# Latent attention in a two-layer fp32 block: the rope's halves swapped by ScalarE, the softmax issued later, the score passes regrouped

## The chip, the cores and the metric

The kernel runs on one core of one Trainium2 chip. The metric is the device time of one execution in microseconds. The profile shows one execution, with its span (first to last instruction) and the granted clock of TensorE as a share of full speed (2.4 GHz; the lower level is 1.2 GHz).

## The reference

A sequence of 512 tokens of width 1024 passes two layers. The first has an attention with forget gates ("fox"), the second a latent attention ("MLA") with 16 heads, and each is followed by a feed-forward part with a short convolution. The change is in the latent attention:

```python
def apply_rope(x, cos, sin):
    x1, x2 = jnp.split(x, 2, axis=-1)
    return jnp.concatenate([x1 * cos - x2 * sin, x1 * sin + x2 * cos], axis=-1)

# shared keys and values: latent (256), one rotated key (64) for all heads
ckv = rmsnorm(x, kv_in_g) @ w_dkv
latent = rmsnorm(ckv[..., :KV_LORA], kv_norm_g)
k_rope = apply_rope(ckv[..., KV_LORA:], cos, sin)
k_nope = latent @ w_uk            # 16 heads of 128
v = latent @ w_uv                 # 16 heads of 128
# queries: 16 heads of 128 + 64 rotated
q = rmsnorm(h @ w_dq, q_norm_g) @ w_uq
sc = (q_nope @ k_nope.T + q_rope @ k_rope.T) * scale
sc = where(visible in chunks of 64, sc, -inf)
o = softmax(sc) @ v
```

All is in fp32.

## The kernel before

Every product is made of parts: an operand is kept as a high part in TensorE's fp32r format and a low part (the rest), and `mm3` issues three passes, high by high, high by low, low by high (lines 84, 85, 86). A pass streams up to 512 columns. The work is written in Python and unrolled; a scheduler orders each engine's queue, mostly as in the text, but an instruction that is ready earlier can go ahead of an earlier one that is not. Buffers rotate in pools, and an instruction waits until its buffer is free. The weights of a projection go through `load_w`: a DMA on SP's queue, a cast to the high part on ScalarE (L105) and a subtraction for the low part on POOL or VectorE (L106). Three raw buffers and two of each part stand ready.

PSUM has eight banks: three in the pool `acc` for projections and outputs, five in the pool `att` for scores and transposes. A bank is evacuated by a ScalarE operation for the high part and a VectorE operation for the low part (`split_ps`, L641 and L642).

Before the head loop the kernel projects the queries' latents (six tiles, `qc`), the rotated key (`krt`) and the keys' latents (two tiles), normalises them (`latents`, L628 and L190), and makes the rope part of the queries for heads 0 and 1 (`mm_rope(0)`), the plain queries of heads 0 and 1, the rotated key's high and low part (`mr`, L742 and L743) and the keys of heads 0 and 1.

The head loop runs over 16 heads, with the scores of head h+1 made while head h is finished. Two heads share one rope projection and one value projection, so the work comes in pairs:

- Even head: scores of the next head (20 passes, L208: per query tile of 128 rows three passes for the plain part and two for the rotated part, against 128, 256, 384 or 512 keys); `mm_rope` for the next pair (18 passes); `proj_v` (24 passes of 256 columns, L687 to L689, four tiles, each evacuated by L690 on ScalarE and L691 on VectorE); `turn`, the rotation; `attn_pT`, ten transposes of the current head's weights (L227), evacuated by L230 on ScalarE and L231 on VectorE; `split_rot`, the two parts of the rotated queries `tr` (L666 ScalarE, L667 VectorE); one key projection (6 passes); `mvalues` (12 passes, L709, of which the last four need the low halves of the transposes).
- Odd head: scores of the next head, a query projection, transposes, a key projection, a second query projection, values.

The softmax of a score tile is in the same function as its passes: a VectorE operation adds the mask and finds the row's maximum (L211), ScalarE makes the exponentials with their sum (L213), and VectorE scales by the reciprocal (L215, L217). `rope` swaps the two halves of each rotated group of 64 rows while it multiplies: four products of 32 partitions, one on POOL and three on VectorE (L637), with the cosine product on POOL (L634) and the sum on VectorE (L638).

Of the kernel before, what the change touches and what calls it, by code (L numbers as in the profile page):

```python
# [42 lines left out]
ROPE_POOL = (0,)  # L43
# [3 lines left out]
def tile_kernel(ctx, tc, xT_d, gains_d, bf_d, const_d, conv_d, wv_d, wq_d, wk_d, wfo_d,  # L47
# [31 lines left out]
    def f(ap):  # L79
        return ap.bitcast(F32)  # L80
# [116 lines left out]
    def attn_scores(p_pool, passes, mask):  # L197

        nm = T(p_pool, [P, NT], F32, "nm", 2)
        l = T(p_pool, [P, NT], F32, "l", 2)  # L200
        rl = T(p_pool, [P, 16], F32, "rl", 2)[:, :NT]
        es = []
        for i in range(NT):
            n = (i + 1) * P
            s_ps = att()
            mms = passes(i, n)
            for j, (lt, rt) in enumerate(mms):
                pe.matmul(s_ps[:, :n], lt, rt, start=(j == 0), stop=(j == len(mms) - 1))  # L208

            e = T(p_pool, [P, n], F32, f"e{i}", 2)  # L210
            v.tensor_tensor_reduce(out=e, in0=s_ps[:, :n], in1=mask[:, S - n:], scale=-1.0, scalar=BIG,  # L211
                                   op0=ALU.add, op1=ALU.min, accum_out=nm[:, i:i + 1])
            a.activation(e, e, AF.Exp, scale=-1.0, bias=nm[:, i:i + 1], accum_out=l[:, i:i + 1])  # L213
            es.append(e)
        v.reciprocal(rl, l)  # L215
        for i in range(NT):
            v.tensor_scalar(out=es[i], in0=es[i], scalar1=rl[:, i:i + 1], scalar2=None, op0=ALU.mult)  # L217
        return es
# [172 lines left out]
    with tc.tile_pool(name="fx", bufs=1, reuse_waits="tile") as fp:  # L391
# [150 lines left out]
        def scores(h):  # L542
            (t1, t2), (m1, m2) = qs.pop(h), ks.pop(h)

            def passes(i, n):
                sl = slice(i * P, (i + 1) * P)
                return [(t1[:, sl], m1[:, :n]), (t2[0:68, sl], m2[0:68, :n])]

            return attn_scores(fp, passes, mask)
# [60 lines left out]
    with tc.tile_pool(name="ml", bufs=1, reuse_waits="tile") as mp:  # L610
# [19 lines left out]

        def rope(A):

            c, t_ = r2(), r2()
            g.tensor_tensor(out=c, in0=A, in1=cosT, op=ALU.mult)  # L634
            for i in range(4):
                o, x = slice(32 * i, 32 * i + 32), slice(32 * (i ^ 1), 32 * (i ^ 1) + 32)
                (g if i in ROPE_POOL else v).tensor_tensor(out=t_[o], in0=A[x], in1=sinT[x], op=ALU.mult)  # L637
            v.tensor_tensor(out=A, in0=c, in1=t_, op=ALU.add)  # L638

# [16 lines left out]
        def turn(pt):  # L656
            A = r2()
            a.activation(A, pt, AF.Copy, scale=MSCALE)
            rope(A)
            return A  # L660
# [33 lines left out]
        def mscores(h):  # L694
# [7 lines left out]
            return attn_scores(mp, passes, mask)  # L702
# [19 lines left out]
        krt = r2()  # L722
# [4 lines left out]
        latents(0, KQ - 2, Rq, G_Q)  # L727
        down(wdkv_d[1], G_KVIN, qc[:, KQ + 1, :])
# [6 lines left out]
        pt = mm_rope(0)  # L735
# [3 lines left out]
        split_rot(0, turn(pt))  # L739
        proj_q(1)  # L740
        rope(krt)
        a.copy(mr[:, 0, :], krt)  # L742
        v.tensor_tensor(out=mr[:, 1, :], in0=krt, in1=f(mr[:, 0, :]), op=ALU.subtract)  # L743
# [17 lines left out]
        es = {0: mscores(0)}  # L761
        proj_k(2)
        proj_q(2)
        for h in range(MH):
            more = h + 2 < MH
            if h + 1 < MH:
                es[h + 1] = mscores(h + 1)
            if h % 2 == 0:
                if more:
                    pt = mm_rope(h // 2 + 1)  # L770
                proj_v(h // 2)
                if more:
                    A = turn(pt)
            elif more:
                proj_q(h + 2)
# [4 lines left out]
            if more and h % 2 == 0:  # L780
                split_rot(h // 2 + 1, A)
            if h + 3 < MH:
                proj_k(h + 3)
                if h % 2:
                    proj_q(h + 3)
# [9 lines left out]
def _constants():  # L795
# [12 lines left out]
    c[:, C_SIN:C_SIN + S] = np.concatenate([sin, -sin] * 2)  # L808
# [72 lines left out]
```

## Time and profile before

| | us |
|---|---|
| median of 3 runs | 1429.17 (1429.05 to 1430.08) |
| the profiled execution | 1429.15 |
| its span | 1427.1 |
| TensorE busy in the span | 1384.2 |
| VectorE busy in the span | 902.9 |
| ScalarE busy in the span | 636.5 |
| POOL busy in the span | 310.6 |

The granted clock is 0.983 over the span. Matmuls are pipelined, and their busy time counts overlaps, so the distance between the starts of two passes tells more than the length of one. The profile's chain of waits follows back from the last instruction what released each step; its lines give the start of a piece, its length and its work.

### The profile page before, as it was taken

Reading aid. Unit: us, or ns where it says so; the run is one execution under the profiler, and the core shown is the slowest. Engines: PE = TensorE matmul, PEld = TensorE weight load, DVE = VectorE, ACT = ScalarE, POOL = GpSimd, SP = SyncE. Lnnn points to the kernel's source line nnn. Section 1 sums busy time; section 2 is a strip of 40 time slices with the busy share of each in tenths; the row PEclk is TensorE's granted clock in tenths of the full one; section 3 lists DMA queues with packets and bytes.
Section 4 is the critical chain, followed back from the end, with each engine's and each line's share of the span. In section 5 each row is a group of like instructions: output and inputs, shape, how many; then the busy total and the mean of one; then the engine's idle time right before and its main releaser. Section 6 shows DMA issues by size and latency. Waiting matters only on the chain.

```text
span 1427.1 us, 17362 instructions
## 1 busy us (share of the span) xinstructions
PE 1384.2 (97%) x6594; PEld 1162.8 (81%) x6594; DVE 902.9 (63%) x1495; ACT 636.5 (45%) x1103; POOL 310.6 (22%) x228
## 2 busy tenths in 40 slices
PE   7999999899999999999799999999999999999997
PEld 7888887788888888888678888888888888888886
DVE  6667786677776744445876666665557777774333
ACT  5588884254444432223454555543225444442111
POOL 4333322400000002154533333321310000000222
PEclk9999999999999999999999999999999999999998
DMA  5321112222323233332111111212232323323331
GB/s 178 102 76 61 51 51 68 89 96 96 103 90 104 89 92 97 106 105 80 50 49 48 59 49 52 61 54 89 89 104 89 104 91 101 98 94 93 96 97 69
DMA packets 41251, 120.22 MB, mean 84 GB/s; under 512 B 5552, under 2 KB 9952, under 8 KB 41168
## 3 DMA queue, kind: packets, MB, share of 16 engines
q1 hardware_dynamic: 39184, 117.00, 25.8%
q0 software_dynamic: 1840, 2.09, 0.6%
q8 instruction: 51, 0.84, 0.2%
q14 instruction: 32, 0.26, 0.1%
q10 hardware_dynamic: 144, 0.03, 0.0%
HBM read 116.74 MB, written 2.36 MB: 83 GB/s over the span
## 4 chain that ended last, share of the span: by engine, by line
PE 85%; DVE 8%; ACT 3%; issue 3%; DMA 1%; POOL 1%; SPq 0%; DVEq 0%; POOLq 0%; ACTq 0%
PE acc L84 24%; PE acc L86 23%; PE acc L85 23%; PE att L208 6%; DVE r L637 2%; PE acc L556 1%; PE att L227 1%; PE acc L709 1%; DVE r L638 1%; DVE ptl L231 1%; DVE big L190 1%; ACT whi L105 1%; DVE tr L667 1%; PE att L84 1%; PE att L86 1%
## 5 line engine op out<-in xcount | busy, mean ns | idle before, releaser
L86 PE MATMUL acc<-big,wlo 128*128 128x512 f32 (+1 forms) x1504 | 584.9, 389 | 7.5 <-POOL wlo L106 3.9
L84 PE MATMUL acc<-big,whi 128*128 128x512 f32 (+1 forms) x1504 | 587.5, 391 | 3.1 <-ACT big L189 2.2
L85 PE MATMUL acc<-big,whi 128*128 128x512 f32 (+1 forms) x1504 | 584.5, 389 | 0.3 <-DVE big L190 0.3
L105 ACT CAST whi<-raw 128x1024 fp32r<-128x1024 f32 (+4 forms) x243 | 229.3, 944 | 427.7 <-PE acc L85 267.5
L86 PEld LDWEIGHTS acc<-big,wlo 128*128 128x128 f32 x1504 | 283.8, 189 | 67.9 <-POOL wlo L106 5.8
L84 PEld LDWEIGHTS acc<-big,whi 128*128 128x128 f32 x1504 | 283.7, 189 | 61.0 <-ACT big L189 2.8
L85 PEld LDWEIGHTS acc<-big,whi 128*128 128x128 f32 x1504 | 283.8, 189 | 58.2 <-DVE big L190 0.6
L106 DVE TENSOR_TENSOR wlo<-raw,whi 128x1024 fp32r<-128x1024 f32 (+3 forms) x179 | 236.2, 1320 | 141.0 <-ACT whi L105 138.3
L142 POOL TENSOR_TENSOR r<-xT 128x512 f32<-128x512 f32 x28 | 31.4, 1124 | 735.9 <-DVE xT L254 414.5
L106 POOL TENSOR_TENSOR wlo<-raw,whi 128x768 fp32r<-128x768 f32 (+3 forms) x64 | 111.8, 1749 | 223.1 <-ACT whi L105 197.3
L294 DVE SCALAR_TENSOR_TENSOR c<-u,conv,c 128x510 f32<-128x510 f32 (+1 forms) x176 | 131.1, 747 | 3.5 <-ACT c L292 0.6
L289 DVE TENSOR_TENSOR u<-acc,R 128x512 f32<-128x512 f32 x88 | 60.3, 687 | 76.3 <-PE acc L86 76.3
L213 ACT ACTIVATE e<-e,nm 128x128 f32<-128x128 f32 (+3 forms) x128 | 71.3, 557 | 43.1 <-DVE nm L211 42.1
L146 POOL TENSOR_TENSOR r<-r,r 128x512 f32<-128x512 f32 x38 | 72.1, 1898 | 27.7 <-ACT r L140 21.0
L292 ACT ACTIVATE c<-u,conv 128x512 f32<-128x512 f32 x88 | 71.4, 813 | 3.1 <-DVE u L289 2.7
L298 ACT ACTIVATE sg<-c 128x512 f32<-128x512 f32 x44 | 27.8, 632 | 78.9 <-DVE c L294 78.8
L231 DVE TENSOR_TENSOR ptl<-att,pth 128x512 fp32r<-128x512 f32 (+3 forms) x128 | 55.4, 481 | 3.4 <-ACT pth L230 2.6
L186 ACT CAST big<-sg 128x512 fp32r<-128x512 f32 x32 | 19.9, 621 | 81.7 <-DVE sg L299 81.6
L230 ACT CAST pth<-att 128x512 fp32r<-128x512 f32 (+3 forms) x128 | 46.9, 435 | 4.8 <-PE att L227 4.3
L208 PE MATMUL att<-kn,tn 128*128 128x128 f32 (+2 forms) x192 | 47.7, 364 | 0.0
L217 DVE TENSOR_SCALAR e<-e,rl 128x128 f32<-128x128 f32 (+3 forms) x128 | 43.0, 399 | 1.1
L254 DVE TENSOR_TENSOR xT<-acc,xT 128x512 f32<-128x512 f32 x20 | 13.8, 691 | 42.5 <-PE acc L86 42.5
(180 smaller groups left out, 1563.8 us busy)
## 6 DMA issues: line engine op xcount, KB each, us to landing
raw<-in_wfi SPq DMA_DIRECT2D x88, 512.0 KB, 3.5
raw<-in_wfu SPq DMA_DIRECT2D x32, 512.0 KB, 3.5
raw<-in_wmo SPq DMA_DIRECT2D x16, 512.0 KB, 3.6
raw<-in_wfu SPq DMA_DIRECT2D x16, 384.0 KB, 3.1
raw<-in_wuqn SPq DMA_DIRECT2D x16, 384.0 KB, 3.0
raw<-in_wq SPq DMA_DIRECT2D x8, 512.0 KB, 3.5
raw<-in_wk SPq DMA_DIRECT2D x8, 512.0 KB, 3.4
raw<-in_wv SPq DMA_DIRECT2D x8, 384.0 KB, 3.1
```

Of the source, the lines that this page charges most:

```text
L84: pe.matmul(out, wh, xh, start=start, stop=False)
L85: pe.matmul(out, wh, xl, start=False, stop=False)
L86: pe.matmul(out, wl, xh, start=False, stop=stop)
L105: a.copy(hi[:, c], raw[:, c])
L106: (eng or v).tensor_tensor(out=lo[:, c], in0=raw[:, c], in1=f(hi[:, c]), op=ALU.subtract)
L146: (adder or g).tensor_tensor(out=self.sum, in0=self.sum, in1=sq, op=ALU.add)
L208: pe.matmul(s_ps[:, :n], lt, rt, start=(j == 0), stop=(j == len(mms) - 1))
L213: a.activation(e, e, AF.Exp, scale=-1.0, bias=nm[:, i:i + 1], accum_out=l[:, i:i + 1])
L231: v.tensor_tensor(out=lo, in0=pt[:, :w], in1=f(hi), op=ALU.subtract)
L289: v.tensor_tensor(out=u, in0=pt, in1=R, op=ALU.mult)
L292: a.activation(c, u, AF.Identity, scale=cw[:, 2:3], bias=cw[:, 3:4])
L294: v.scalar_tensor_tensor(out=c[:, s:], in0=u[:, :S - s], scalar=cw[:, 2 - s:3 - s], in1=c[:, s:], op0=ALU.mult, op1=ALU.add)
```

## The change

Four things are changed.

- The rotation: the halves are swapped by four ScalarE copies of 32 partitions each, out of the PSUM bank of the rope projection into SBUF (`swapped`). VectorE multiplies the bank by the cosine with the scale, and later the swapped tile by the sine and adds the two. POOL has no part in it. `turn` returns a function `end`, which issues the last two operations. For the rotated key, the copies are from SBUF and the two products and the sum are on POOL; they are issued between two projections of the keys' latents, and the key's two parts (POOL for the low one) follow before the first rope projection. The key and its swapped copy lie in a buffer of the pool `kn`.
- The order in the loop: at an even head `mm_rope` and the first part of `turn` come before the next head's scores, and `proj_v` and `end` come after the transposes.
- The softmax is split off `attn_scores`: the mask and maximum of all four tiles stay with the scores, and the exponentials, the reciprocal and the scaling are issued behind the transposes of the current head. In the first layer's attention the same function is called right away.
- The passes: the four score tiles are opened at once. In the latent attention the plain passes of all four tiles come first and the rotated passes of all four after them.

```diff
@@ attn_scores
-        es = []
+        es, pts = [], [att() for _ in range(NT)]
+        for i, j, first, last, lt, rt in passes():
+            pe.matmul(pts[i][:, :(i + 1) * P], lt, rt, start=first, stop=last)
         for i in range(NT):
             n = (i + 1) * P
-            s_ps = att()
-            mms = passes(i, n)
-            for j, (lt, rt) in enumerate(mms):
-                pe.matmul(s_ps[:, :n], lt, rt, start=(j == 0), stop=(j == len(mms) - 1))
             e = T(p_pool, [P, n], F32, f"e{i}", 2)
-            v.tensor_tensor_reduce(out=e, in0=s_ps[:, :n], in1=mask[:, S - n:], scale=-1.0, scalar=BIG,
+            v.tensor_tensor_reduce(out=e, in0=pts[i][:, :n], in1=mask[:, S - n:], scale=-1.0, scalar=BIG,
                                    op0=ALU.add, op1=ALU.min, accum_out=nm[:, i:i + 1])
-            a.activation(e, e, AF.Exp, scale=-1.0, bias=nm[:, i:i + 1], accum_out=l[:, i:i + 1])
             es.append(e)
-        v.reciprocal(rl, l)
-        for i in range(NT):
-            v.tensor_scalar(out=es[i], in0=es[i], scalar1=rl[:, i:i + 1], scalar2=None, op0=ALU.mult)
-        return es
+
+        def softmax():
+            for i in range(NT):
+                a.activation(es[i], es[i], AF.Exp, scale=-1.0, bias=nm[:, i:i + 1], accum_out=l[:, i:i + 1])
+            v.reciprocal(rl, l)
+            for i in range(NT):
+                v.tensor_scalar(out=es[i], in0=es[i], scalar1=rl[:, i:i + 1], scalar2=None, op0=ALU.mult)
+
+        return es, softmax
+
+    def by_tile(of, order=None):
+        every = [of(i, (i + 1) * P) for i in range(NT)]
+        m = len(every[0])
+        for js in (order or (range(m),)):
+            for i in range(NT):
+                for j in js:
+                    yield (i, j, j == 0, j == m - 1, *every[i][j])
@@ rotation
-        def rope(A):
-            c, t_ = r2(), r2()
-            g.tensor_tensor(out=c, in0=A, in1=cosT, op=ALU.mult)
+        def swapped(dst, src, sc):
             for i in range(4):
                 o, x = slice(32 * i, 32 * i + 32), slice(32 * (i ^ 1), 32 * (i ^ 1) + 32)
-                (g if i in ROPE_POOL else v).tensor_tensor(out=t_[o], in0=A[x], in1=sinT[x], op=ALU.mult)
-            v.tensor_tensor(out=A, in0=c, in1=t_, op=ALU.add)
+                a.activation(dst[o], src[x], AF.Copy, scale=sc)
...
         def turn(pt):
-            A = r2()
-            a.activation(A, pt, AF.Copy, scale=MSCALE)
-            rope(A)
-            return A
+            c, t_ = r2(), r2()
+            swapped(t_, pt, MSCALE)
+            v.scalar_tensor_tensor(out=c, in0=pt, scalar=MSCALE, in1=cosT, op0=ALU.mult, op1=ALU.mult)
+
+            def end():
+                v.tensor_tensor(out=t_, in0=t_, in1=sinT, op=ALU.mult)
+                v.tensor_tensor(out=c, in0=c, in1=t_, op=ALU.add)
+                return c
+
+            return end
@@ mscores
-            return attn_scores(mp, passes, mask)
+            return attn_scores(mp, lambda: by_tile(passes, (range(3), range(3, 5))), mask)
@@ before the loop
-        krt = r2()
+        kr = T(mp, [P, 2, S], F32, "kn", 2)
+        krt, krs = kr[:, 0, :], kr[:, 1, :]
         down(wdkv_d[KL], G_KVIN, krt)
...
         latents(0, KQ - 2, Rq, G_Q)
+        swapped(krs, krt, 1.0)
+        g.tensor_tensor(out=krt, in0=krt, in1=cosT, op=ALU.mult)
+        g.tensor_tensor(out=krs, in0=krs, in1=sinT, op=ALU.mult)
+        g.tensor_tensor(out=krt, in0=krt, in1=krs, op=ALU.add)
         down(wdkv_d[1], G_KVIN, qc[:, KQ + 1, :])
...
-        pt = mm_rope(0)
+        a.copy(mr[:, 0, :], krt)
+        g.tensor_tensor(out=mr[:, 1, :], in0=krt, in1=f(mr[:, 0, :]), op=ALU.subtract)
+        end = turn(mm_rope(0))
...
-        split_rot(0, turn(pt))
+        split_rot(0, end())
         proj_q(1)
-        rope(krt)
-        a.copy(mr[:, 0, :], krt)
-        v.tensor_tensor(out=mr[:, 1, :], in0=krt, in1=f(mr[:, 0, :]), op=ALU.subtract)
@@ head loop
         for h in range(MH):
-            more = h + 2 < MH
+            more, even = h + 2 < MH, h % 2 == 0
+            if even and more:
+                end = turn(mm_rope(h // 2 + 1))
             if h + 1 < MH:
-                es[h + 1] = mscores(h + 1)
-            if h % 2 == 0:
-                if more:
-                    pt = mm_rope(h // 2 + 1)
-                proj_v(h // 2)
-                if more:
-                    A = turn(pt)
-            elif more:
+                begin(h + 1)
+            if not even and more:
                 proj_q(h + 2)
...
             pT = attn_pT(mp, es.pop(h))
-            if more and h % 2 == 0:
-                split_rot(h // 2 + 1, A)
+            if even:
+                proj_v(h // 2)
+                if more:
+                    split_rot(h // 2 + 1, end())
+            if h + 1 < MH:
+                softmax[h + 1]()
             if h + 3 < MH:
                 proj_k(h + 3)
@@ _constants
-    c[:, C_SIN:C_SIN + S] = np.concatenate([sin, -sin] * 2)
+    c[:, C_SIN:C_SIN + S] = np.concatenate([-sin, sin] * 2)
```

`begin(h)` calls `mscores(h)` and keeps the weights' tiles and their `softmax`.

## Rows read from the trace of the kernel before

**Rows 1.** The page's parts 1 and 4: busy time; the chain's shares by engine.

```profile
PE 1384.2 (97%) x6594; PEld 1162.8 (81%) x6594; DVE 902.9 (63%) x1495; ACT 636.5 (45%) x1103; POOL 310.6 (22%) x228
...
PE 85%; DVE 8%; ACT 3%; issue 3%; DMA 1%; POOL 1%; SPq 0%; DVEq 0%; POOLq 0%; ACTq 0%
```

**Rows 2.** Windows: us, busy of PE, PEld, DVE, ACT, POOL; clock, DMA, GB/s.

```profile
679.62:694.75 15.13, 12.66 (x46) 9.87 (x44) 9.56 (x20) 4.89 (x7) 5.76 (x4) 0.77 0.09 27
694.75:723.49 28.74, 21.68 (x97) 17.44 (x96) 23.92 (x36) 13.51 (x29) 14.85 (x10) 0.94 0.21 61
756.15:790.32 34.17, 32.99 (x176) 28.59 (x174) 21.48 (x50) 17.77 (x44) 12.44 (x8) 0.95 0.16 50
790.32:803.68 13.36, 12.24 (x71) 10.40 (x70) 10.27 (x20) 7.33 (x18) 6.24 (x4) 1.00 0.18 60
803.68:808.74 5.06, 5.00 (x23) 4.59 (x23) 3.59 (x10) 2.58 (x9) 1.21 (x1) 0.66 0.23 52
808.74:821.28 12.54, 12.54 (x65) 10.59 (x64) 5.82 (x14) 5.92 (x14) 4.86 (x3) 1.00 0.14 42
```

**Rows 3.** Chain of waits over one pair: start us, us, what.

```profile
787.25 3.23 PE att L208 x20
...
799.99 1.88 DVE r L638
...
819.58 1.87 PE acc L709 x12
```

**Rows 4.** Timeline of PE, one pair, last column the wait.

```profile
794.42 0.28 PE L687 MATMUL acc<-whi,big 128*128 128x256 f32 x1
...
797.53 1.25 PE L227 MATMUL att<-idf,e 128*128 128x128 f32 x10
...
800.02 1.39 PE L709 MATMUL acc<-pth,Vp 128*128 128x512 f32 x8
...
802.52 1.32 PE L709 MATMUL acc<-ptl,Vp 128*128 128x512 f32 x4 [1.12 <-DVE ptl L231]
```

**Rows 5.** Single lines: count, ns shortest/median/longest, first and last start, shape.

```profile
L658 ACT ACTIVATE r<-acc x8: 592/592/608, 696.0 to 931.6; 128x512 f32<-128x512 f32 x8
...
L666 ACT CAST tr<-r x12: 615/616/618, 767.7 to 939.4; 64x512 fp32r<-64x512 f32 x12
...
L642 DVE SCALAR_TENSOR_TENSOR tn<-acc,tn x12: 690/692/692, 752.2 to 950.8; 128x512 fp32r<-128x512 f32 x12
...
L638 DVE TENSOR_TENSOR r<-r,r x9: 679/1883/1890, 704.3 to 936.8; 128x512 f32<-128x512 f32 x9
...
L634 POOL TENSOR_TENSOR r<-r,cosT x9: 1282/1742/1747, 698.6 to 932.4; 128x512 f32<-128x512 f32 x9
```

**Rows 6.** Windows of one pair, exponentials (L213) alone: busy us, count.

```profile
787.25:821.45 34.20, 5.03 (x16) 0.95 0.17 51
```

**Rows 7.** Timelines of DVE, POOL and ACT, one pair, by start.

```profile
797.94 0.76 DVE L691 TENSOR_TENSOR Vp<-acc,Vp 128x256 fp32r<-128x256 f32 x2
...
799.14 2.18 POOL L106 TENSOR_TENSOR wlo<-raw,whi 128x768 fp32r<-128x768 f32 x1
...
801.79 1.67 DVE L231 TENSOR_TENSOR ptl<-att,pth 128x512 fp32r<-128x512 f32 x4
...
815.33 0.88 ACT L105 CAST whi<-raw 128x768 fp32r<-128x768 f32 x1
...
816.28 1.85 POOL L106 TENSOR_TENSOR wlo<-raw,whi 128x768 fp32r<-128x768 f32 x1 [0.67 <-ACT whi L105]
```

**Rows 8.** Waits of PE, 679.62 to 723.5: us in total, times, longest.

```profile
PE acc L84 <- ACT big L189: 2.2, 1, 2.2
...
PE acc L86 <- POOL wlo L106: 3.9, 2, 2.0
...
PE att L208 <- ACT mr L742: 3.1, 1, 3.1
```

**Rows 9.** Timeline of POOL before the head loop.

```profile
708.16 4.38 POOL L106 TENSOR_TENSOR wlo<-raw,whi 128x768 fp32r<-128x768 f32 x2
```

More of the change, by code (lines that the diff above doesn't have):

```diff
@@ L42 @@
 FIN_POOL = (6, 7)
-ROPE_POOL = (0,)
 @with_exitstack
@@ L547, in passes @@
                 return [(t1[:, sl], m1[:, :n]), (t2[0:68, sl], m2[0:68, :n])]
-            return attn_scores(fp, passes, mask)
+            es_h, softmax = attn_scores(fp, lambda: by_tile(passes), mask)
+            softmax()
+            return es_h
         def values(h, pT, op_t):
@@ L759, in fill, with begin @@
                 next(ahead[d][1])
-        es = {0: mscores(0)}
+        es, softmax = {}, {}
+        def begin(h):
+            es[h], softmax[h] = mscores(h)
+        begin(0)
+        softmax[0]()
         proj_k(2)
@@ L779, in tile_kernel @@
             pT = attn_pT(mp, es.pop(h))
-            if more and h % 2 == 0:
-                split_rot(h // 2 + 1, A)
+            if even:
[4 more added lines that the diff above has]
+                softmax[h + 1]()
             if h + 3 < MH:
                 proj_k(h + 3)
-                if h % 2:
+                if not even:
                     proj_q(h + 3)
```

## The prediction

> **What bounds the kernel now.** I read the page's busy shares and chain first. TensorE is busy for 97% of the span and holds 85% of the chain; VectorE holds most of the rest [rows 1]. So only time in which TensorE stands, or runs below full clock, can be won, and the next view is the windows, cut at the places the change touches. Before the head loop the reader sees two bad stretches: 15.13 us at clock 0.77 and 28.74 us at 0.94 with 21.68 us of matmuls. Inside the loop a pair of heads takes 34.17 us. The odd half has none of the loss: from its weight passes to its values it is 12.54 us long with 12.54 us of matmul. All the loss lies in the even half and in the scores behind it [rows 2].
>
> The timeline of PE shows where. In the even half the rope projection (18 passes, 790.32 to 794.42) and the value projection are followed at 797.53 by the transposes and, after one small key projection, at 800.02 by the values of the head. Their second part starts only at 802.52, after a wait of 1.12 us for the low halves of the transposed weights [rows 2, 4]. The chain says why: VectorE was at the rope's last addition for 1.88 us from 799.99, and the low halves came behind it in its queue [rows 3]. The next scores then run at clock 0.66 and take 5.06 us [rows 2], while undisturbed scores take 3.23 [rows 3].
>
> **What can be won in a pair.** Values: from 800.02 to 803.68 is 3.66 us, undisturbed 1.87 [rows 3, 4], so 1.79 lost. Scores: 5.06 - 3.23 = 1.83 lost. Together 3.62 us. The first pair's rope starts at 723.49 and the second's at 756.15, 32.66 us apart and so 1.51 less than 34.17 [rows 2]; there only 2.1 is to be had. Seven pairs have a rope, so 6 x 3.62 + 2.1 = 23.8 us.
>
> **What the change puts there**, on a clock that starts with the rope's first pass in an even half. TensorE: rope to 4.1, scores of the next head to 7.3, transposes to 8.4, value projection to 11.5, key projection to 13, values to 14.8; then the next scores, of which three passes of five (about 2 us) come before the first that needs the new rotated queries. These are due at 16.8.
>
> ScalarE: one copy out of PSUM (592 ns) becomes four of a quarter of the partitions and the same length. The trace has no such copy. The nearest are 592 ns for 128 partitions from PSUM and 616 for 64 from SBUF, so partitions do not make it shorter, and a quarter of 592 (148) is the floor. I take 0.59 [rows 5]: 1.8 us more a pair (bounds 0 and 1.9). It is hidden if ScalarE has room: it works 17.77 us of 34.17 [rows 2], so 19.5 of about 31 after. In the even half alone it has 7.33, plus 1.8, plus one head's half of the 5.03 of exponentials [rows 6]: 11.6 of 14.8. Copies run from 4.4 to 6.9.
>
> VectorE: the three 32-partition products and the add go, and POOL's two products. In come one product from PSUM (as the 0.69 of L642), one product and one sum of 128x512 in SBUF, each 0.68 at best and 1.88 at worst by L638's own spread [rows 5]. The product from PSUM shares its bank with the four copies; I let it wait for them, to 6.9, and the score reductions queue behind it. The last reduction has its scores at 7.5; with 0.69 for each of the longest operations these are done by 9. Then come the four low halves of the transposes, 1.67 us, until 10.9 with the hand-over from ScalarE; then the low halves of four value tiles, 0.42 each [rows 7], until 13 with a gap near 12; in the gap and behind it the rope's product and sum, until 13.8; then ScalarE's casts (0.62 each) and the first subtraction, 15.1. That is 1.7 us before 16.8. The low transposes are 3.3 us early for the values' second part at 14.2. So both losses go. The price: the value projection's four tiles share three PSUM banks with the rope, so its fourth waits until VectorE has read the first, which now stands behind the transposes' low halves. I estimate 0.5 us more than now (bounds 0 and 1: none of VectorE's 1.67 stands in the way, or most of it). Net 3.1 us a pair and 1.6 in the first: 20.2 us.
>
> The softmax is issued later, but its exponentials have until the next head's transposes, a whole head of TensorE work (12 us or more) away; the reductions are not moved. That costs nothing; without the cover it is 2.5 us of exponentials a head [rows 6] and the scaling behind them. Regrouping the passes changes neither their number nor their shapes, so nothing; four PSUM banks of five are open at once, and the last transposes need the third back at 8.3, about when its reduction ends. The first layer's attention shares the function, but there each engine gets the same instructions in the same order: nothing.
>
> The rope moves ahead of the scores, and with it the load on SP, ScalarE's cast and POOL's low part of its weights. It is moved past no other load, so the order of loads stays. The split now ends in the odd half at 818.13, and the rope would start at 821.28 [rows 2, 7]: 3.1 us of slack, so nothing.
>
> **Before the loop.** The 28.74 us hold 54 projection passes at 0.228 (18 in 4.10), two scores of 3.23 and a broadcast of 0.45: 19.2. So 9.5 us are lost: 3.9 waiting for weights' low parts on POOL, 3.1 for the rotated key [rows 8], and 2.5 in restarts and clock. POOL does the splits that are waited for between rope products, and ends two of them after 4.38 us [rows 9], where one takes 1.85 alone [rows 7]. After the change the key is turned before the last projection of the latents, and POOL has no part in the queries' rope. I count 8 back, bounds 5 and 9.5.
>
> In the 15.13 us before it, the turned key puts three POOL operations of 1.28 to 1.75 us each, and a subtraction, near the latents. TensorE already waits 2.2 us there for a latent [rows 8]. I take 1 us lost; the bounds are 3.6 (three latent products stretched by 1.2 as L638 is) and a gain of 1.5 (most of that 2.2), since the key no longer holds one of four scratch buffers.
>
> **Sum.** 20.2 + 8 - 1 = 27.2 us off the profiled execution's 1429.15 us, which is the median (1429.17) to 0.02 us: 1402.0. With the bounds of each term (per pair 0.5 to either side; 3 us less or 1.5 more for the stretch before the loop, 2.6 and 2.5 for the one before it) this case reaches from 1394 to 1411.
>
> **A rule against it.** The product and the sum at the rope's end read two SBUF operands. L638 shows 0.68 us and 1.88 for one shape [rows 5]; the one at 799.99 ran beside a split that POOL began at 799.14 and needed 2.18 us for [rows 3, 7]. The Trainium skill, "SBUF — State Buffer", section "Who interferes with whom", says that a VectorE instruction with two SBUF inputs contends with GpSimd reading SBUF, while one with a single SBUF input does not. This trace agrees: the L642 form, from PSUM, never leaves 0.69 [rows 5]. By that rule both of the new operations can be stretched by POOL's split of the next query weights, and the sum would be that of the first rival.
>
> **Rivals.** (1) The rotated queries are still late. For it: two operations stretched by 1.2 us each move 15.1 to 17.5, past 16.8, and a ScalarE queue in another order can add more. Against it: POOL's split lasts about 2 us and meets one of them rather than both. A stall of 0.7 to 2 us, with the scores again at the low clock (1.83), takes 2.5 to 3.1 of the 3.1 won. The loop then gives 0 to 4 us and the time is 1418 to 1422; where some pairs escape, from 1410.
>
> (2) Slower: the rope weights are not ready. If the cast is issued only behind the values' evacuation at the end of the odd head, TensorE waits for some 0.6 of that (L658's 592 ns), 0.88 of the cast and 1.85 of the low part [rows 5, 7]: 3.3 us a pair, and 1.8 of clock behind it, 5.1 against 3.1 won. Seven pairs at 5.1 on top of the 1402.0: about 1438. It decides from 4.3 us of loss a pair (27.2 and the 2.9 below, over seven). Against it stand the 3.1 us of slack and the unchanged order of loads.
>
> (3) The change doesn't do what it says: the order in the text is not that of the queues, and the old wait comes back under another name, with the gains before the loop lost on POOL: within 3 us of 1429.
>
> **Chances.** Forecast 0.66, rival 1 0.22, rival 2 0.05, rival 3 0.04; 0.03 for gains above the forecast's range. No change is within 0.2%, 2.9 us, which is about what a measurement can tell. Faster 0.91, same 0.04, slower 0.05. The range takes the forecast with its bounds, the larger gains down to 1391 and rival 1 up to 1417, and leaves out the rest.
>
> **What would show it.** Values that follow the key projection without a wait for low halves; scores at clock 1.00 and 3.2 us; pairs of about 31 us; the 28.74 us near 21; copies of 0.59; no wait of PE for the rotated key. A wait of the scores for "tr" with the clock down means rival 1, a wait for "wlo" at the head of the even half rival 2. The prediction is wrong most easily where a queue's order differs from my walk, on VectorE above all.

## The result and the profile after

The changed kernel takes 1410.74 us (median of 4 runs, 1410.36 to 1411.27), beside 1429.62 (median of 4, 1429.05 to 1431.79) for the kernel before; the ratio of the means is 0.9865, with a 95% interval of 0.9848 to 0.9883. The forecast was 1402.0 with a range of 1391 to 1417. The direction was right, and so was most of the mechanism; of 27.2 us that were to come back, 18.9 did. The profiled execution's span is 1408.8, and so 18.3 under that of before; the accounts below are made on the spans.

The page's busy time answers to [rows 1]. TensorE now has 98% of its span, and the other engines have what the change gave or took: ScalarE 12.2 us more, POOL 28.4 less.

```profile
PE 1373.6 (98%) x6594; PEld 1150.8 (82%) x6594; DVE 886.6 (63%) x1482; ACT 648.7 (46%) x1131; POOL 282.2 (20%) x214
```

The windows answer to [rows 2]: first the stretch that took 15.13 us, then the one of 28.74, then six pairs from the first pass of rope(1) to that of rope(7), one pair, and the scores behind its even half.

```profile
681.67:697.81 16.14, 14.03 (x54) 10.18 (x53) 10.85 (x21) 7.90 (x13) 6.55 (x5) 0.89 0.13 36
697.81:715.94 18.13, 15.99 (x67) 12.78 (x68) 11.78 (x29) 9.79 (x21) 5.70 (x4) 0.91 0.20 63
715.94:908.14 192.20, 187.60 (x1046) 160.25 (x1044) 122.01 (x294) 114.11 (x277) 52.16 (x37) 1.00 0.18 56
780.02:812.01 31.99, 31.22 (x176) 26.72 (x175) 20.33 (x49) 18.94 (x46) 8.49 (x6) 1.00 0.17 54
796.38:799.61 3.23, 3.23 (x19) 2.73 (x19) 3.15 (x6) 0.63 (x2) 0.74 (x1) 1.00 0.61 190
```

Two lines of PE's timeline of the kernel before are needed beside them, the scores of head 1 and the first pass of rope(7):

```profile
720.32 0.45 PE L208 MATMUL att<-kn,tn 128*128 128x128 f32 x3
...
927.15 0.40 PE L84 MATMUL acc<-big,whi 128*128 128x512 f32 x1
```

In the stretch of 28.74 us the scores of head 1 stood ahead of rope(1); they began at 720.32 and now come behind it. So 18.13 us answer to 720.32 - 694.75 = 25.57, which is 7.4 less. The stretch ahead of it became 1.0 longer, and it began 2.05 later (681.67 for 679.62): together 4.4 before the loop.

The two windows don't hold the same work, though. Their border is the second broadcast, and that has moved: the kernel before issues 36 projection passes ahead of it and 54 behind, the changed one 45 and 45. Nine passes at 0.227 us are 2.0 us. So for the same passes I estimate that the first stretch became 1.0 shorter and the second 5.4.

The six pairs took 927.15 - 723.49 = 203.66 and take 192.2, 11.5 less. From rope(7) to the end it was 1427.1 - 927.15 = 499.95 and is 1408.8 - 908.14 = 500.7, of which 3.2 are scores that the kernel before had ahead of rope(7): 2.5 less. The sum is 18.4. A pair has gone from 34.17 to 32.0, where 31.1 were forecast, and the scores take 3.23 at clock 1.00, where they took 5.06 at 0.66 (three of their twenty passes now stand earlier, as the next view shows).

The timeline of PE over the even half answers to [rows 4].

```profile
779.86 0.45 PE L83 MATMUL acc<-big,whi 128*128 128x512 f32 x1
...
784.03 2.07 PE L203 MATMUL att<-kn,tn 128*128 128x128 f32 x12
785.95 1.45 PE L203 MATMUL att<-mr,tr 128*128 128x128 f32 x8
787.23 1.78 PE L237 MATMUL att<-idf,e 128*128 128x128 f32 x10
788.77 0.36 PE L703 MATMUL acc<-whi,big 128*128 128x256 f32 x1
...
790.99 0.45 PE L203 MATMUL att<-kn,tn 128*128 128x128 f32 x3
792.14 0.38 PE L703 MATMUL acc<-whi,big 128*128 128x256 f32 x1 [0.70 <-DVE Vp L707]
...
794.34 1.38 PE L725 MATMUL acc<-pth,Vp 128*128 128x512 f32 x8
795.56 0.81 PE L725 MATMUL acc<-ptl,Vp 128*128 128x512 f32 x4
...
797.89 1.54 PE L203 MATMUL att<-mr,tr 128*128 128x128 f32 x8
```

The values' second part follows the first without a wait; the 1.12 us for the low halves are gone, and the clock over the six pairs is 1.00. But there are two new places. The transposes take 788.77 - 787.23 = 1.54 us, where they took 798.54 - 797.53 = 1.01, and V's fourth tile comes only at 792.14, with three passes of the next scores pulled into the gap. The waits of the weight loads (PEld) show both, and some that the passes hide, from 715 to 950 (us in total, times, longest; `nm` are the row maxima that the reductions write, `tr` the rotated queries):

```profile
PEld acc L703 <- DVE Vp L707: 6.1, 8, 0.8
PEld att L237 <- DVE nm L208: 3.8, 14, 0.3
PEld att L203 <- DVE tr L683: 2.0, 6, 0.3
```

Why these come is seen on the two engines that empty the banks. VectorE's timeline of the same half (start, us, last column the idle time before it):

```profile
786.91 0.69 DVE L669 SCALAR_TENSOR_TENSOR r<-acc,cosT 128x512 f32<-128x512 f32 x1 [5.53 <-ACT r L647]
787.51 0.28 DVE L208 CUSTOM_DVE_ANT_0 e<-att,R 128x128 f32<-128x128 f32 x1
...
788.54 0.69 DVE L208 CUSTOM_DVE_ANT_0 e<-att,R 128x512 f32<-128x512 f32 x1
...
790.07 1.68 DVE L241 TENSOR_TENSOR ptl<-att,pth 128x512 fp32r<-128x512 f32 x4 [0.23 <-ACT pth L240]
791.67 1.22 DVE L707 TENSOR_TENSOR Vp<-acc,Vp 128x256 fp32r<-128x256 f32 x3
792.81 0.68 DVE L673 TENSOR_TENSOR r<-r,r 128x512 f32<-128x512 f32 x1
...
794.10 2.47 DVE L217 TENSOR_SCALAR e<-e,rl 128x128 f32<-128x128 f32 x3
796.61 1.95 DVE L683 TENSOR_TENSOR tr<-r,tr 64x512 fp32r<-64x512 f32 x2
```

And ScalarE's:

```profile
784.48 2.39 ACT L647 ACTIVATE r<-acc 32x512 f32<-32x512 f32 x4
787.84 0.40 ACT L214 ACTIVATE e<-e,nm 128x128 f32<-128x128 f32 x1 [0.96 <-DVE nm L208]
...
789.45 1.41 ACT L240 CAST pth<-att 128x512 fp32r<-128x512 f32 x4
```

VectorE is idle for 5.53 us ahead of the cosine product, the last 2.4 of them for the four copies. The reductions stand behind that product in the queue, and when they begin, at 787.51, the passes of all four score tiles have ended (785.95 + 1.45 = 787.40). Three exponentials of the next head (787.84 to 789.43) run ahead of the copies of the transposed weights, though in the text they are issued behind them. So the low halves `ptl` come at 790.07 and V's at 791.67, and only then is a bank free for V's fourth tile.

Before the loop the kernel spreads a reciprocal root over all rows twice (a broadcast): VectorE makes eight products, and TensorE sums them. The first broadcast serves the queries' latents, the second the keys'. VectorE shows the products of both (L171), and POOL the three operations on the key beside the first.

```profile
667.62 0.69 DVE L635 TENSOR_TENSOR kn<-acc,R 128x512 f32<-128x512 f32 x1 [2.63 <-PE acc L85]
...
671.02 4.81 DVE L171 TENSOR_SCALAR r<-idf,two 128x128 fp32r<-128x128 f32 x8
...
695.11 0.69 DVE L669 SCALAR_TENSOR_TENSOR r<-acc,cosT 128x512 f32<-128x512 f32 x1 [4.68 <-ACT r L647]
695.72 1.15 DVE L171 TENSOR_SCALAR r<-idf,two 128x128 fp32r<-128x128 f32 x3
```

In the kernel before the same products took 1.66 and 1.65 us, and the second eight came at 689.91, not 695.72:

```profile
670.93 1.66 DVE L172 TENSOR_SCALAR r<-idf,two 128x128 fp32r<-128x128 f32 x8
...
689.91 1.65 DVE L172 TENSOR_SCALAR r<-idf,two 128x128 fp32r<-128x128 f32 x8
```

POOL of the changed kernel:

```profile
671.23 1.29 POOL L746 TENSOR_TENSOR kn<-kn,cosT 128x512 f32<-128x512 f32 x1 [0.52 <-ACT kn L647]
672.47 1.29 POOL L747 TENSOR_TENSOR kn<-kn,sinT 128x512 f32<-128x512 f32 x1
673.84 1.32 POOL L748 TENSOR_TENSOR kn<-kn 128x512 f32<-128x512 f32 x1
```

### The profile page after: what moved, and what is told of

It is laid out like the page before. It is cut to its first block, busy times and chain, and to the rows that moved or that the text cites. A ratio compares the mean times of both kernels' runs of the same rounds, so it can differ in the third digit from the quotient of the medians.

```text
span 1408.8 us, 17333 instructions
## 1 busy us (share of the span) xinstructions
PE 1373.6 (98%) x6594; PEld 1150.8 (82%) x6594; DVE 886.6 (63%) x1482; ACT 648.7 (46%) x1131; POOL 282.2 (20%) x214
## 5 line engine op out<-in xcount | busy, mean ns | idle before, releaser
L104 ACT CAST whi<-raw 128x1024 fp32r<-128x1024 f32 (+5 forms) x243 | 229.2, 944 | 413.8 <-PE acc L84 281.6
L105 POOL TENSOR_TENSOR wlo<-raw,whi 128x768 fp32r<-128x768 f32 (+3 forms) x64 | 108.0, 1687 | 251.1 <-ACT whi L104 205.5
L217 DVE TENSOR_SCALAR e<-e,rl 128x128 f32<-128x128 f32 (+3 forms) x128 | 55.7, 495 | 1.2
L237 PE MATMUL att<-idf,e 128*128 128x128 f32 x320 | 43.5, 275 | 0.5
L237 PEld LDWEIGHTS att<-idf,e 128*128 128x128 f32 x320 | 36.9, 140 | 8.5 <-DVE nm L208 3.8
```

Source lines behind the costliest of these rows:

```text
L104: a.copy(hi[:, c], raw[:, c])
L105: (eng or v).tensor_tensor(out=lo[:, c], in0=raw[:, c], in1=f(hi[:, c]), op=ALU.subtract)
L237: pe.transpose(out=pt[:, (i - j) * P:(i - j + 1) * P], in_=es[i][:, j * P:(j + 1) * P], identity=idf)
```

## The experiments

All start from the changed kernel (1410.74). They were made in four groups, and the kernel before, run beside each, had medians of 1428.8 to 1429.8; differences of about 1 us are therefore not read as effects. The profiled executions reach the eviction of the rotated key (667.62 above) up to 1.7 us apart, with nothing changed ahead of it, so two distances are given that this does not enter: A, from that eviction's start to the first pass of V in the head loop, and B, from there to the last such pass, seven pairs later. A comes out at 55.9 to 57.2 in the seven runs in which nothing ahead of the first scores was changed, so only what leaves this span counts. B is 225.7 in all three runs that leave the loop alone. For the changed kernel both are read from the view of V's line (count; ns shortest, median, longest; first and last start), as 724.8 - 667.62 and 950.5 - 724.8.

```profile
L703 PE MATMUL acc<-whi,big x64: 277/283/389, 724.8 to 950.5; 128*128 128x256 f32 x64
```

| run | us, median (lowest to highest) | A | B |
|---|---|---|---|
| changed kernel | 1410.74 (1410.36 to 1411.27) | 57.2 | 225.7 |
| softmax early | 1413.19 (1411.81 to 1414.34) | 56.2 | 227.7 |
| by tile | 1407.86 (1406.85 to 1409.70) | 56.5 | 223.2 |
| cosine first | 1406.03 (1404.98 to 1406.78) | 53.9 | 223.2 |
| exponentials held | 1407.59 (1407.05 to 1409.15) | 56.1 | 222.2 |
| rope alone | 1409.17 (1407.51 to 1410.52) | 55.9 | 224.7 |
| key late | 1410.66 (1407.92 to 1411.55) | 56.3 | 225.7 |
| by tile, held | 1406.98 (1406.78 to 1407.68) | 55.9 | 222.8 |
| four edits | 1401.20 (1400.61 to 1402.20) | 52.3 | 219.5 |
| V in two banks | 1407.13 (1406.04 to 1408.36) | 57.1 | 220.8 |
| five edits | 1400.23 (1396.06 to 1401.45) | 54.9 | 215.9 |
| five, broadcast first | 1397.53 (1397.00 to 1398.08) | 52.3 | 215.9 |
| broadcast first | 1408.41 (1406.78 to 1409.30) | 54.3 | 225.7 |

**Softmax early** undoes the move of the softmax.

```diff
-            es[h], softmax[h] = mscores(h)
+            es[h], sm = mscores(h)
+            sm()
+            softmax[h] = lambda: None
```

> The changed kernel with one of its three parts undone: each head's exps and scalings are issued right behind its reductions again, not behind the transposes of the head before. Theory: the part does nothing by itself, because in the changed kernel three of the four exps of the next head already stand ahead of the transposed weights' copies on ScalarE; the time stays within 2 us of 1410.7 and the passes of V still wait 0.7 to 0.9 us for their fourth tile. Rival: the move is what keeps the pair at 32.0 us; undone, all four exps and their reciprocal stand ahead of the transposes, the values come 1 us later in each of 7 pairs, and the time is 1416 to 1420 us.

It is 2.5 us slower, beyond the theory's 2 and short of the rival. The fourth exponential now stands between the first and the second copy of the transposed weights; the scheduler pulls twelve passes of the next scores ahead of V's fourth tile instead of three, and TensorE waits inside them for a bank that `ptl` holds (PE's timeline):

```profile
791.31 1.73 PE L203 MATMUL att<-kn,tn 128*128 128x128 f32 x9
793.77 0.96 PE L203 MATMUL att<-kn,tn 128*128 128x512 f32 x3 [0.72 <-DVE ptl L241]
```

So the move does something, by one exponential of four.

**By tile** undoes the regrouping of the passes.

```diff
-            return attn_scores(mp, lambda: by_tile(passes, (range(3), range(3, 5))), mask)
+            return attn_scores(mp, lambda: by_tile(passes), mask)
```

> The changed kernel with the regrouping of the score passes undone: the five passes of a tile stand together, so the first pass with rotated queries comes 9 passes earlier, right behind the first tile's three. Theory: the rotated queries are ready about 1.5 to 2 us after the odd head's scores begin, so a wait of 1 to 1.5 us comes back in each of 7 pairs, and some of the passes behind it run at the lower clock: 1418 to 1428 us. Rival: the copies out of PSUM alone make the rotated queries early enough; no wait of more than 0.3 us, and the time stays within 2 us of 1410.7.

Neither range holds: it is 2.9 us faster. The rival's mechanism does, since no wait for `tr` is left in the loop. Tile by tile the reductions of the first tiles run under the passes of the later ones, and the transposes take the 1.25 us of ten passes that [rows 4] show, without a wait. The rotated queries are early: their sum, at 792.81 with regrouping, is done before `ptl` (VectorE, then PE):

```profile
788.71 0.69 DVE L673 TENSOR_TENSOR r<-r,r 128x512 f32<-128x512 f32 x1
789.31 1.68 DVE L241 TENSOR_TENSOR ptl<-att,pth 128x512 fp32r<-128x512 f32 x4
```

```profile
786.71 1.25 PE L237 MATMUL att<-idf,e 128*128 128x128 f32 x10
...
791.37 0.39 PE L703 MATMUL acc<-whi,big 128*128 128x256 f32 x1 [0.97 <-DVE Vp L707]
```

What is left is V's fourth tile, 0.97 instead of 0.70; that the sum now stands ahead of `ptl` fits this, and no run tests it alone.

**Cosine first** puts VectorE's product from the bank ahead of the four copies.

```diff
-            swapped(t_, pt, MSCALE)
             v.scalar_tensor_tensor(out=c, in0=pt, scalar=MSCALE, in1=cosT, op0=ALU.mult, op1=ALU.mult)
+            swapped(t_, pt, MSCALE)
```

> The changed kernel with one line moved: VectorE's product with the cosine stands ahead of the four ScalarE copies in program order (both read the same bank). Theory: VectorE's reductions of the even head wait behind that product, which waits for ScalarE's copies, and so the transposes wait 0.5 us for a bank; with the product first the reductions follow the scores at once, that wait is gone, the pair takes 31.5 us, and the time is 1406 to 1408 us. Rival: the bank is what both need, the copies move back by the product's 0.7 us, and the rotated queries become late by as much: 1410 to 1415 us, with a wait for tr ahead of the odd head's rope passes.

4.7 us faster, at the lower end of the theory's range. The reductions follow the scores, and no wait for `nm` is left:

```profile
782.40 0.69 DVE L668 SCALAR_TENSOR_TENSOR r<-acc,cosT 128x512 f32<-128x512 f32 x1 [2.85 <-PE acc L85]
784.48 0.29 DVE L208 CUSTOM_DVE_ANT_0 e<-att,R 128x128 f32<-128x128 f32 x1 [1.39 <-PE att L203]
```

B shrinks by 2.5, under the forecast 0.5 a pair, as the waits for `tr` and for V's bank grow, from 2.0 to 2.6 and from 6.1 to 6.5 us in all. The other part is A, 53.9 and so 2.0 under the lowest of the span, which no expectation had: before the loop the second broadcast's products had stood behind the same product, ahead of which VectorE was idle for 4.68 us (the line at 695.11 above).

**Exponentials held** queues the next head's exponentials behind the last copy of the transposed weights.

```diff
...
-            a.copy(hi, pt[:, :w])
+            last_hi[0] = a.copy(hi, pt[:, :w])
...
-                softmax[h + 1]()
+                with tc.issue_after(last_hi[0].ins):
+                    softmax[h + 1]()
```

> The changed kernel with the exps of the next head held behind the last copy of the transposed weights on ScalarE. Theory: V's fourth tile waits 0.7 us for a bank because three exps run ahead of the copies of the transposed weights, whose low halves stand ahead of V's low halves on VectorE; held back, the copies begin 1.5 us earlier, the wait for the bank falls under 0.2 us, and the time is 1404 to 1407 us. Rival: VectorE's late reductions hold the low halves, not the exps: the wait for the bank stays over 0.5 us, and the time stays within 2 us of 1410.7, or the held exps make the odd head's transposes late and it is slower.

3.1 us faster, 0.6 short of the theory's range and outside the rival's. The copies start 0.63 us behind the first transpose instead of 2.22 (ScalarE), and V's fourth tile waits 0.38 (PE), not under 0.2:

```profile
786.55 1.50 ACT L242 CAST pth<-att 128x512 fp32r<-128x512 f32 x4 [0.99 <-PE att L239]
```

```profile
785.92 1.78 PE L239 MATMUL att<-idf,e 128*128 128x128 f32 x10
...
790.51 0.39 PE L705 MATMUL acc<-whi,big 128*128 128x256 f32 x1 [0.38 <-DVE Vp L709]
```

The transposes' 3.8 us for `nm` stay, and the wait for `tr` is gone as well.

**Rope alone** joins softmax early and by tile.

> The rope part of the change by itself: the copies out of PSUM and the merged scaling, with the softmax issued right behind its reductions and the score passes tile by tile, both as before. Theory: the rope part carries all of the gain, the regrouping by itself costs 2 to 3 us and the moved softmax gives 2 to 3 us: 1409 to 1412 us, with no wait for tr in the loop. Rival: the two other parts are needed for the rope part to pay (the rotated queries become late, or V's tiles do): 1416 us or more.

As the theory has it: 1409.17. With the other three it makes a square: regrouped and moved 1410.7, regrouped alone 1413.2, moved alone 1407.9, neither 1409.2. Regrouping costs 2.9 to 4.0 us; the moved softmax gives 2.5 with regrouping and 1.3 without, where the two spans overlap (B says the same with less scatter: 2.0 and 1.5). So neither of these two parts is needed for the gain. But what is left in this run is more than the rotation: the new order of the loop (the rope's passes ahead of the scores, V behind the transposes), the key's earlier turn and the four tiles opened together stay. No run parts the swap on ScalarE from the new order, so which of them gives how much of the gain is not shown.

**Key late** takes the key's two products and their sum from POOL to VectorE, behind the second mean of squares, and issues the key's two parts behind them.

```diff
-        g.tensor_tensor(out=krt, in0=krt, in1=cosT, op=ALU.mult)
-        g.tensor_tensor(out=krs, in0=krs, in1=sinT, op=ALU.mult)
-        g.tensor_tensor(out=krt, in0=krt, in1=krs, op=ALU.add)
...
         r = rstd_of([squares.sum], KVL)
+        with tc.issue_after(last_mean[0].ins):
+            v.tensor_tensor(out=krt, in0=krt, in1=cosT, op=ALU.mult)
+            v.tensor_tensor(out=krs, in0=krs, in1=sinT, op=ALU.mult)
+            v.tensor_tensor(out=krt, in0=krt, in1=krs, op=ALU.add)
```

> The changed kernel with the key's three products and sum taken from GpSimd to VectorE and placed behind the second mean of squares, where VectorE stood idle for 4.7 us at 690.4; the split of the rotated key follows them. Theory: the eight 128x128 products of the first reciprocal root's broadcast took 4.81 us because the key's three GpSimd instructions ran beside them; without these they take 1.3 to 1.7 us, the last pass group of the down projection starts 1.5 to 2 us earlier, and the time is 1408.5 to 1409.5 us. Rival: the products are slow there for another reason (their operand, VectorE's queue), and keep 3 us or more: no change, 1410 to 1411.5 us.

The mechanism is the theory's, the time the rival's (VectorE):

```profile
669.26 0.69 DVE L637 TENSOR_TENSOR kn<-acc,R 128x512 f32<-128x512 f32 x1 [2.62 <-PE acc L85]
...
672.66 1.66 DVE L173 TENSOR_SCALAR r<-idf,two 128x128 fp32r<-128x128 f32 x8
675.65 0.69 DVE L637 TENSOR_TENSOR big<-acc,R 128x512 f32<-128x512 f32 x1 [1.33 <-PE acc L85]
```

The products are back at 1.66, and the next eviction comes 6.39 us after the key's, not 8.14. But the time does not change, and A, 56.3, stays inside the span of the unchanged runs: the second broadcast's products start 696.26 - 669.26 = 27.0 us behind the key's eviction, again behind the first rope's cosine product.

**Broadcast first** tests that by itself: the second broadcast's products ahead of that product.

```diff
...
-        end = turn(mm_rope(0))
+        pt0 = mm_rope(0)
         r = rstd_of([squares.sum], KVL)
+        Rk = bcast(r, T(mp, [P, S], F32, "e3", 2))
+        with tc.issue_after(last_d[0].ins):
+            end = turn(pt0)
         proj_q(0)
-        latents(KQ, KL, bcast(r, T(mp, [P, S], F32, "e3", 2)), G_KV)
+        latents(KQ, KL, Rk, G_KV)
```

> The changed kernel with that one order alone: the second broadcast's products ahead of the first rope's cosine product on VectorE, everything else as it is. Theory: in the changed kernel VectorE stood idle from 690.4 to 695.1 with these products behind the cosine product; ahead of it the 1.25 and 0.88 us that TensorE waits for the key's latents, and the lower clock behind them, are gone, and the stretch from the eviction at 667.62 to V's first pass at 724.8 falls from 57.2 to 54 us: 1406.5 to 1408.5 us. Rival: the first rope is then late for the first scores by as much: 1410 to 1411.5 us.

A is 54.3, where the theory had 54, and the time, 2.3 us less, is in its range. The products start 690.81 - 668.10 = 22.7 us behind the key's eviction, instead of 28.1 (VectorE):

```profile
690.81 1.65 DVE L173 TENSOR_SCALAR r<-idf,two 128x128 fp32r<-128x128 f32 x8
```

**By tile, held**, and **four edits**, which adds cosine first and key late:

> Regrouping undone and the next head's exps held behind the transposed weights' copies. Theory: the two waits are separate; without regrouping the reductions of the first tiles run under the last tile's passes, so no transpose waits, and held exps give V's fourth tile its bank: the two gains add up, no wait of the loop over 0.5 us each pair, 1404 to 1406 us. Rival: with the exps held the softmax of the odd head comes late, or the fourth tile of V still waits 1 us for VectorE as in the kernel without regrouping: 1407 to 1409 us.

> All four edits together: regrouping undone, the product with the cosine first, exps held, the key's products on VectorE behind the second mean. Theory: against the kernel without regrouping and with held exps, the product first gives at most 1 us more and the key's turn 1.5 us: 1401.5 to 1404 us, and the pair takes 31.0 us or less. Rival: with regrouping undone the earlier product with the cosine puts VectorE's queue in another order and gives the transposes or V a new wait: 1404 to 1407 us.

The first came out at the lower edge of its rival's range: the gains of 2.9 and 3.1 us don't add, they give 3.8. The exponentials are out of ScalarE's way, but VectorE still waits 1.10 us for the four copies ahead of the cosine product, and V's fourth tile still waits 0.97. With the product first (four edits) V's wait is 0.49, B falls by another 3.3, and the time is a little under the theory's. The key's edit lies ahead of the loop and left B at 225.7 by itself, so B's share is the product's.

**V in two banks** lets two tiles of 256 columns share a bank, with one copy and one subtraction for both.

```diff
-            for t in range(NT):
-                o = acc()[:, :2 * MV]
+            for u in range(NT // 2):
+                two = acc().rearrange("p (t c) -> p t c", t=2)
+                for t in (2 * u, 2 * u + 1):
+                    o = two[:, t % 2, :]
...
+                a.copy(Vp[:, t2, 0, :], two)
+                v.tensor_tensor(out=Vp[:, t2, 1, :], in0=two, in1=f(Vp[:, t2, 0, :]), op=ALU.subtract)
```

> The changed kernel with V's four tiles in two banks instead of four: two 256-column tiles share one, and the copies and low halves take both at once. Theory: what V's fourth tile waits for is one of three accumulator banks, not VectorE's low half as such; with two banks no pass of V waits, the values' wait for the low half of V does not come in its place (they stand 1.5 us of transposed weights behind), and 0.6 to 0.8 us in each of 8 pairs are back: 1404.5 to 1406.5 us. Rival: the low halves of V are late because VectorE is late; without the wait for the bank the values wait for them instead, 0.5 us or more: 1409 to 1411 us.

V's passes wait for nothing, and B falls by 4.9, the time by 3.6. The values' wait for V's halves does come in part, which the theory had denied (waits of the weight loads):

```profile
PEld acc L728 <- DVE Vp L710: 4.5, 14, 0.5
...
PEld acc L728 <- ACT Vp L709: 1.6, 7, 0.2
```

The time, 1407.13, lies between the two ranges. **Five edits** joins it to the four, and **five, broadcast first** adds the broadcast's order, with the key's products behind the broadcast too:

> The four edits together and V's tiles in two banks. Theory: the wait for the bank that was left in each pair, 0.6 us of the weight load's, is gone: 1396.5 to 1398.5 us. Rival: the values' passes wait for V's low halves in its place: 1400 to 1402 us.

> The five edits together, with the second broadcast's products put ahead of the first rope's cosine product and of the key's products on VectorE. Theory: in the run with the five edits the second broadcast's eight products stood behind the cosine product, which waited for the first rope's passes and for ScalarE; ahead of it they start at about 691, the latents come 3 to 4 us earlier, and the 54.9 us from the eviction of the rotated key (669.30) to V's first pass become 51 to 52.5 us: 1395 to 1397.5 us. Rival: the latents then wait for ScalarE or the rotated queries come late for the first scores, and the stretch stays over 54 us: 1399 us or more.

Five edits has B 3.6 under that of four edits, but its median came out in the rival's range, and only 1.0 under four edits, with one run at 1396.06: the values do wait for V's halves in part (3.1 us in 7), and A went back from 52.3 to 54.9. The second broadcast's products came at 696.26, 4.6 us later behind the key's eviction than in four edits; they stood behind a cosine product ahead of which VectorE was idle for 2.58 us. Why the queues differ there the runs don't show. With the broadcast put first A is 52.3, and the time 1397.53, just above the theory's range; the ratio of the means to the kernel before is 0.9781 (0.9759 to 0.9804). That is 13.2 us under the changed kernel with the same number of passes on TensorE.

## Why the prediction was right, and where its sizes were off

**What can be won in a pair: right.** The 1.79 us of the values and the 1.83 of the slow scores are both gone. Rope alone shows that neither the moved softmax nor the regrouping is needed for it; the swap and the new order are not parted.

**The price of 0.5 us a pair: too small.** It was put on V's fourth tile alone. Of 3.62 us, 34.17 - 32.0 = 2.2 came back, so the price is 1.4. The weight loads' waits say of what: V's fourth tile 6.1 us in 8 (0.76 each), the transposes 3.8 in 14 (two a pair, 0.54 together), the rotated queries 2.0 in 6 (0.33), less the 0.4 that such waits for V and `tr` cost before (1.7 us in 9, 1.4 in 7): 1.2. Three steps failed:

- The walk ended the transposes' low halves at 10.9; they ended at 791.75 - 779.86 = 11.9, on a clock that starts with the rope's first pass at 779.86. It let the exponentials come behind the copies, as in the text, and three of four ran ahead. Holding them gave 3.5 us in B.
- "The last transposes need the third back at 8.3, about when its reduction ends": it ended at 788.62 - 779.86 = 8.8 and the fourth at 9.4, and the even half's transposes waited twice, 0.54 us together; the odd half's didn't wait. The walk had VectorE's product behind the copies and the reductions behind the product, and priced that at nothing. Cosine first took that wait away.
- Regrouping was to cost nothing, as neither the number nor the shapes of passes change. It costs 2.9 us or more, because all four reductions come due at once in the even half, just ahead of the transposes. The product's place and the regrouping are two causes of the same wait: by tile and cosine first each take all of it away.

**The rotated queries: in time, but in part by luck.** They were to be ready at 15.1 and needed at 16.8. The first subtraction, 1.23 of the 1.95 us that begin at 796.61, ended at 797.84, 18.0 on that clock, and the passes that need it began then (797.89), after a wait of 0.3. So the margin of 1.7 us was gone, and the wait stayed that short because TensorE was itself 0.9 late. The windows show the clock at 1.00. The product and the sum, which the rule against it named, took 0.68 each, as POOL's split began only at 794.34. It met the scalings of the weights instead, which the walk did not have there: 2.47 us for three, where four take 1.27 with POOL idle,

```profile
803.03 1.27 DVE L217 TENSOR_SCALAR e<-e,rl 128x128 f32<-128x128 f32 x4
```

and the next split met the first subtraction (1.23 us, the second 0.69). The third scaling alone took 2.01 us beside the split, and 0.41 at 803.5. So the cause of rival 1 came, on other operations, and cost 2.0 us in six waits and not 2.5 to 3.1 in each pair.

**The softmax at no cost: right as far as it goes.** It even gives 2.5 us here, which was not forecast.

**The copies at 0.59 and the rope's weights: right.** The copies take 2.39 us for four, and TensorE waits nowhere over 0.4 us for a low part of weights in the loop (1.3 us in 6).

**Before the loop: 8 forecast, about 5.4 measured; -1 forecast, about -1 measured, by luck.** For the same passes the stretch of 15.13 us became 1.0 shorter, near the better bound, and began 2.05 later: the key's POOL operations had moved ahead of it, beside the products of the first broadcast, which went from 1.66 to 4.81 us. The walk had these operations beside the latents. Key late shows that they were the cause.

The step that failed is the term of 8 in the stretch of 28.74 us, which gave back the waits for POOL and the key and put nothing against them. It left out VectorE's queue: the second broadcast's products stood behind the first rope's cosine product, 695.72 for 689.91, TensorE waited 1.25 and 0.88 us for the latents behind it, and the window's clock is 0.91. Broadcast first shows it: with the products ahead A is 1.6 under the span of the unchanged runs, and the time 2.3 us less. The sign "the 28.74 us near 21" seems met, 18.13 and 3.2 of scores, but only because nine passes had gone into the stretch ahead. With both causes mended, and cosine first besides, A is 52.3, 3.6 to 4.9 shorter.

**The sum.** Of 27.2 - 18.3 = 8.9 us missing, 2.6 are before the loop, 5.6 the six pairs (5 x 3.1 + 1.6 = 17.1 for 11.5) and 0.6 the last pair, each rounded. Rivals 2 and 3 did not happen. The price of 1.4 us a pair lies outside its own bounds of 0 and 1; the time, 1410.74, stays just inside the reach that the forecast gave itself (1394 to 1411), as no other term went to its worse bound.

## What to carry to other kernels

When a change moves an instruction, walk each engine's real queue and not the text: an operation that waits for another engine holds everything behind it, and here one product in front of four reductions and eight small multiplications cost 4.7 us, found by moving one line. Evacuate first what others share (the bank, the reductions, the copies that free a bank), and put what has slack, as the exponentials, behind it by an explicit edge. Before moving work to an idle engine look at what it will stand beside, also ahead of the stretch that is being improved.

## What the runs showed of the hardware

A multiplication by a per-row scalar, with one SBUF tile as its operand, was stretched beside POOL as far as an operation with two (0.68 to 1.88 in [rows 5]): eight of 128x128 took 4.81 us beside three POOL operations, and 1.66 when these were gone, while POOL's own took 1.29 to 1.32, against a shortest of 1.28 in [rows 5]. The Trainium skill, "SBUF — State Buffer", section "Who interferes with whom", lists a multiplication by a scalar, beside copies and casts, among the operations that can take the port pair shared with GpSimd. This trace agrees. The prediction had drawn only on that section's rule for two SBUF operands, and its words that an operation with one does not contend left out the section's condition, that VectorE is not in a mode that takes both port pairs.

A ScalarE copy of 32 partitions from PSUM takes 0.59 us (587 to 593 ns in the 32 of the changed kernel), as long as one of 128 (592 ns in [rows 5]).
